# Last quarter of the output projection as one chunk of 512 columns, eight of its weight tiles resident, and a rewritten layer boundary

## The chip, the core and the metric

The kernel runs on one core of a Trainium2 chip. The metric is the device time of one execution in microseconds (us). TensorE multiplies matrices, VectorE and ScalarE do elementwise work, GpSimd does some elementwise work and issues some DMAs, and SyncE issues most DMAs. In profiles they are PE (PEld for its weight loads), DVE, ACT, POOL and SP.

## The reference

Two layers run one after the other on x, 256 tokens by 2048 columns, all in float32. Per layer:

```
h = rms_norm(x, g_pre)
p = h @ w_in                         # 2048 -> 5952 columns
A: 8 query heads, 2 key/value heads, per-head RMS norm, 2-D rotary, softmax attention
B: 4 heads with low-rank q and kv, shared rotary key
C: 4 heads, neighbourhood attention on a 4 x 64 token grid with a learned bias
o = concat(A, B, C) * silu(gate columns of p)
y = o @ w_out                        # 2048 -> 2048
x = x + rms_norm(y, g_post)
```

What matters here is the last two lines of layer 0 and the first line of layer 1: y must be complete along its 2048 columns before its root mean square, and so the new x, is known; and layer 1's projection needs the new x times its norm weight, transposed.

## The kernel before, in words

Every matmul has 128 x 128 stationary operands. A float32 factor is kept as two parts, `hi` (a rounded copy) and `lo` (the rest), and a product is three matmuls: hi x hi, hi x lo, lo x hi (`mm3`, L219). The weights stream: they lie in memory as a list of items of up to 128 x 1024 float32 (512 KB). For each item SyncE loads a `raw` tile (`load`, L262; 4 buffers), ScalarE writes `hi`, VectorE writes `lo` by a subtraction (`conv`, L272, through `split`, L196; 5 buffers of each), and TensorE uses it (`products`, L852). `feed` (L283) keeps loads and conversions ahead of use: a conversion runs up to 4 items ahead, and not further than 5 tiles past the last item that is done with.

Items are grouped in chunks of output columns (`_chunks`, L43). For a layer's input projection the other factor is `hT`, the transposed x, also as hi and lo, one tile of 128 x 16 x 2 x 256. For the output projection it is `oT`, the gated attention output (one tile of hi, one of lo). A chunk of lay-out "T" has the token halves m = 0 and m = 1 (128 tokens each) as two PSUM tiles, and its columns are the moving dimension. The output projection y consists of y0, y1, y2 with 512 columns and y3, y4 with 256 columns; an item holds two k-tiles of 512 columns or four of 256.

As a chunk of y ends, ScalarE takes its sum of squares (`junk`, L338) and VectorE multiplies it by `g_post` (L740). The last chunk, y4, is run by `last_chunk` (L935), where the order is written out by hand: all items for m = 0, then, while TensorE runs the same items for m = 1, the end of the first half: `ends` gives the scale `rs_r` (VectorE `rs_a`, L957; a power on GpSimd, L958), `x_new` gives the residual (`residual`, L767, VectorE, four instructions of 512 columns) and the product with the next layer's norm weight (`x_gain`, L772, GpSimd, four instructions), `x_transpose` transposes it on TensorE (L225, four 128 x 128 blocks to a PSUM tile `tr`, two buffers), and `x_split` writes it as hi (ScalarE) and lo (VectorE) to `hT`. Behind y4 stand the items C[0] to C[5] of layer 1's first chunk (320 columns, three k-tiles to an item, 960 columns): first for m = 0, with the second half's chain in between, then for m = 1. In layer 1 the function writes the residual to the output instead and ends.

The framework schedules instructions by priority and dependences, so an engine's order need not be that of the text; the orders shown below are those of the built programs. Each engine runs its own order strictly and waits on semaphores.

## Time and profile before

| | us |
|---|---|
| median of 3 runs | 825.32 (824.39 to 826.72) |
| profiled execution | 826.01 |
| its span, first to last instruction | 824.2 |
| TensorE busy | 806.8 (98%) |
| VectorE busy | 557.2 (68%) |
| ScalarE busy | 436.7 (53%) |
| GpSimd busy | 52.6 (6%) |
| granted TensorE clock, mean | 0.993 |

An engine's busy time counts its instructions' spans; matmuls overlap and their ends are modelled, so for TensorE the distance between starts tells more than the span of one. A row of the timeline has start, length, engine, line, operation, destination and sources, count, and in brackets the idle time before it with what released it. Times are counted from the first instruction. Layer 0's y2 runs to about 384.9 us, y3 and y4 to 410, and the first chunk of layer 1 to about 433.6.

### The profile page before, as it was taken

Reading aid. Unit: us, or ns where it says so; the run is one execution under the profiler, and the core shown is the slowest. Engines: PE = TensorE matmul, PEld = TensorE weight load, DVE = VectorE, ACT = ScalarE, POOL = GpSimd, SP = SyncE. Lnnn points to the kernel's source line nnn. Section 1 sums busy time; section 2 is a strip of 40 time slices with the busy share of each in tenths; the row PEclk is TensorE's granted clock in tenths of the full one; section 3 lists DMA queues with packets and bytes.
Section 4 is the critical chain, followed back from the end, with each engine's and each line's share of the span. In section 5 each row is a group of like instructions: output and inputs, shape, how many; then the busy total and the mean of one; then the engine's idle time right before and its main releaser. Section 6 shows DMA issues by size and latency. Waiting matters only on the chain.

```text
span 824.2 us, 12380 instructions
## 1 busy us (share of the span) xinstructions
PE 806.8 (98%) x4659; PEld 711.6 (86%) x4659; DVE 557.2 (68%) x871; ACT 436.7 (53%) x765; POOL 52.6 (6%) x63
## 2 busy tenths in 40 slices
PE   8999999999999999999989999999999999999996
PEld 5999888888888888888888998888889888888896
DVE  6567777476786687554686667875767866874544
ACT  6574555454665565454454455655456555554440
POOL 1110000000000000200340000000000000000000
PEclk9999999999999999999989999999999999999998
DMA  8875544654545466665347546446545454556632
GB/s 296 293 290 191 195 164 154 226 189 172 180 144 189 152 209 207 233 230 184 136 180 246 167 167 204 156 151 231 192 163 179 154 180 163 195 199 213 201 130 102
DMA packets 46235, 156.72 MB, mean 190 GB/s; under 512 B 5216, under 2 KB 7392, under 8 KB 46176
## 3 DMA queue, kind: packets, MB, share of 16 engines
q1 hardware_dynamic: 43584, 146.50, 51.7%
q0 software_dynamic: 2592, 9.44, 3.3%
q8 instruction: 36, 0.59, 0.3%
q14 instruction: 23, 0.19, 0.1%
HBM read 151.72 MB, written 4.19 MB: 189 GB/s over the span
## 4 chain that ended last, share of the span: by engine, by line
PE 78%; issue 12%; DVE 3%; DMA 3%; POOL 1%; ACT 1%; SPq 1%; DVEq 0%; POOLq 0%; ACTq 0%
PE mm L216 64%; PE pv L216 5%; PE sc L216 5%; PE tr L225 3%; DVE wlo L201 2%; DMA wraw<-in_wts_dram 1%; DMA u<-in_x_dram 1%; DMA g_akn<-in_akn_dram 1%; PE tr L216 1%; DVE u L767 1%; ACT whi L200 1%; DVE hT L204 0%; ACT junk L338 0%; POOL rs_r L212 0%; POOL s_akn L315 0%
## 5 line engine op out<-in xcount | busy, mean ns | idle before, releaser
L201 DVE TENSOR_TENSOR wlo<-wraw,whi 128x1024 fp32r<-128x1024 f32 (+2 forms) x265 | 321.4, 1215 | 186.8 <-ACT whi L200 182.0
L200 ACT CAST whi<-wraw 128x1024 fp32r<-128x1024 f32 (+2 forms) x265 | 273.4, 1033 | 247.2 <-PE mm L216 202.1
L216 PE MATMUL mm<-whi,hT 128*128 128x512 f32 (+1 forms) x768 | 234.5, 380 | 4.8 <-DVE hT L201 3.5
L216 PEld LDWEIGHTS mm<-whi,hT 128*128 128x128 f32 x768 | 143.1, 190 | 30.6 <-DVE hT L201 3.8
L216 PE MATMUL mm<-whi,oT 128*128 128x512 f32 (+1 forms) x640 | 166.8, 348 | 0.0
L216 PE MATMUL mm<-hT,whi 128*128 128x512 f32 x640 | 161.1, 393 | 0.0
L216 PE MATMUL mm<-wlo,hT 128*128 128x512 f32 (+1 forms) x384 | 145.6, 380 | 0.9 <-DVE wlo L201 0.9
L216 PEld LDWEIGHTS mm<-hT,whi 128*128 128x128 f32 x640 | 115.2, 189 | 20.8
L216 PEld LDWEIGHTS mm<-whi,oT 128*128 128x128 f32 x640 | 112.2, 189 | 14.8
L216 PE MATMUL mm<-wlo,oT 128*128 128x512 f32 (+1 forms) x320 | 108.9, 347 | 0.0
L216 PEld LDWEIGHTS mm<-hT,wlo 128*128 128x128 f32 x640 | 87.3, 190 | 6.3
L216 PE MATMUL mm<-hT,wlo 128*128 128x256 f32 x640 | 89.2, 282 | 0.0
L216 PEld LDWEIGHTS mm<-wlo,hT 128*128 128x128 f32 x384 | 72.8, 190 | 14.1 <-DVE wlo L201 2.6
L216 PEld LDWEIGHTS mm<-wlo,oT 128*128 128x128 f32 x320 | 60.6, 189 | 7.3
L216 PE MATMUL sc<-u,u 128*128 128x256 f32 x224 | 33.7, 290 | 0.0
L212 POOL TENSOR_TENSOR rs_r<-rs_a,mhalf 128x2 f32<-128x2 f32 (+2 forms) x12 | 15.1, 1256 | 281.4 <-DVE rs_a L211 281.4
L678 ACT ACTIVATE pr<-sc,nb,scq 128x256 f32<-128x256 f32 x32 | 17.8, 560 | 25.3 <-DVE nb L673 25.3
L216 PEld LDWEIGHTS sc<-u,u 128*128 128x128 f32 x224 | 29.1, 190 | 0.5
L216 PE MATMUL pv<-pT,u 128*128 128x256 f32 x192 | 28.1, 282 | 0.0
L216 PEld LDWEIGHTS pv<-pT,u 128*128 128x128 f32 x192 | 26.2, 189 | 1.3
L216 PE MATMUL pv<-hT,whi 128*128 128x256 f32 x128 | 23.7, 285 | 0.0
L338 ACT ACTIVATE junk<-mm 128x512 bf16<-128x512 f32 (+1 forms) x20 | 10.2, 508 | 24.8 <-PE mm L216 24.7
(140 smaller groups left out, 763.7 us busy)
## 6 DMA issues: line engine op xcount, KB each, us to landing
wraw<-in_wts_dram SPq DMA_DIRECT2D x247, 512.0 KB, 3.8
wraw<-in_wts_dram SPq DMA_DIRECT2D x10, 480.0 KB, 4.3
u<-in_x_dram SPq DMA_DIRECT2D x4, 512.0 KB, 8.6
u<-in_bias_dram POOLq DMA_DIRECT2D x4, 512.0 KB, 5.0
u<-in_x_dram POOLq DMA_DIRECT2D x4, 512.0 KB, 5.5
u<-in_gpost_dram POOLq DMA_DIRECT2D x4, 512.0 KB, 6.4
x<-u SPq DMA_DIRECT2D x4, 512.0 KB, 2.8
u<-x POOLq DMA_DIRECT2D x4, 512.0 KB, 5.2
```

The lines of the kernel that those rows point to most:

```text
L200: nc.scalar.copy(hi.bitcast(F32R), ps)
L201: nc.vector.tensor_tensor(lo.bitcast(F32R), ps, hi, ALU.subtract)
L212: nc.gpsimd.tensor_tensor(r[:, :m], a[:, :m], self.mhalf[:, :m], ALU.pow)
L216: self.nc.tensor.matmul(out, lhsT=l.bitcast(F32R), rhs=r.bitcast(F32R), start=start, stop=stop, skip_group_check=True)
L225: self.nc.tensor.transpose(out, in_, self.ident)
L338: self.nc.scalar.activation(j[:, :n], src, AF.Square, scale=scale, accum_out=acc)
L678: nc.scalar.activation(pr[:, qt], s3[:, qt], AF.Exp, bias=nb[:, qt:qt + 1], scale=scale, accum_out=sm[:, qt:qt + 1])
L767: self.nc.vector.scalar_tensor_tensor(xc, self.q4(self.yg[m], c), r[:, :1], xc, ALU.mult, ALU.add)
```

## The change

y3 and y4 become one chunk y3 of 512 columns, eight items of two k-tiles. It is now the chunk that `last_chunk` runs, so eight items are used for m = 0 and again for m = 1. `hT` becomes four tiles hT0 to hT3 of 128 x 2048, each holding four k-tiles. Items 0 to 3 of y3 are held: their hi and lo go into these four tiles, which get layer 1's transposed x afterwards. The other items use the usual buffers, and `feed` counts only these ("place"); during y2 it converts up to four items further ahead. `x_gain` runs on VectorE instead of GpSimd. In `last_chunk` the first half's residuals, products, transposes and splits are spread over the eight items of the second pass, and the conversions of layer 1's items are placed by `conv(j)`. `post_y3` is gone, `post_y2` makes the partial sum `ypre` of three chunks, and y3's sum of squares is the fourth.

```diff
--- before
+++ after
@@ -25,6 +25,7 @@
 LO_BUFS = 5
 WARM = 11
 LC = 4
+HELD = 4
 HEAD_EVERY = {"A": 4, "B": 4, "C": 3}
 
 
@@ -72,8 +73,7 @@
         ("y0", "T", "out", np.arange(0, 512), 2),
         ("y1", "T", "out", np.arange(512, 1024), 2),
         ("y2", "T", "out", np.arange(1024, 1536), 2),
-        ("y3", "T", "out", np.arange(1536, 1792), 4),
-        ("y4", "T", "out", np.arange(1792, 2048), 4),
+        ("y3", "T", "out", np.arange(1536, 2048), 2),
     ]
 
 
@@ -113,6 +113,12 @@
         i = own.index(y[0])
         late = [it for it in y if it["ks"][0] >= 12]
         order += own[:i] + [it for it in y if it not in late] + late + own[i + len(y):]
+    place = 0
+    for it in order:
+        j = it["ks"][0] // 2
+        it["held"] = j if it["name"] == "y3" and j < HELD else None
+        it["place"] = place
+        place += it["held"] is None
     return order, off
 
 
@@ -272,8 +278,12 @@
     def conv(self, i):
         it = self.items[i]
         n = it["ncols"]
-        hi = self.pw.tile([P, 1024], F32, tag="hi", name=self.nm("whi"), bufs=HI_BUFS)[:, :it["n"]]
-        lo = self.pw.tile([P, 1024], F32, tag="lo", name=self.nm("wlo"), bufs=LO_BUFS)[:, :it["n"]]
+        if it["held"] is not None:
+            t = self.h_slot(it["held"])
+            hi, lo = t[:, :1024], t[:, 1024:]
+        else:
+            hi = self.pw.tile([P, 1024], F32, tag="hi", name=self.nm("whi"), bufs=HI_BUFS)[:, :it["n"]]
+            lo = self.pw.tile([P, 1024], F32, tag="lo", name=self.nm("wlo"), bufs=LO_BUFS)[:, :it["n"]]
         n1 = n if i == 0 else it["n"]
         for c in range(0, it["n"], n1):
             self.split(it["raw"][:, c:c + n1], hi[:, c:c + n1], lo[:, c:c + n1])
@@ -283,15 +293,19 @@
     def feed(self, cur, done, lc=LC):
 
         n = len(self.items)
-        while self.nconv < min(n, cur + lc + 1, done + HI_BUFS):
-            while self.nload < min(n, self.nconv + RAW_BUFS):
-                self.load(self.nload)
-                self.nload += 1
-            self.conv(self.nconv)
-            self.nconv += 1
+        place = lambda i: self.items[i]["place"]
+        while self.nconv < min(n, cur + lc + 1) and place(self.nconv) < place(done) + HI_BUFS:
+            self.conv_next()
         while self.nload < min(n, self.nconv + RAW_BUFS):
             self.load(self.nload)
             self.nload += 1
+
+    def conv_next(self):
+        while self.nload < min(len(self.items), self.nconv + RAW_BUFS):
+            self.load(self.nload)
+            self.nload += 1
+        self.conv(self.nconv)
+        self.nconv += 1
 
 
     def layer_consts(self, l):
@@ -754,12 +768,9 @@
 
     def post_y2(self, l, ps):
         yield from self.post_y(l, ps, 2, 512, 2)
-
-    def post_y3(self, l, ps):
-        yield from self.post_y(l, ps, 6, 256, 3)
         self.ypre = self.tmp("ypre", [P, 2])
         for m in range(2):
-            self.nc.vector.reduce_sum(self.ypre[:, m:m + 1], self.yss[m][:, :4], AX.X)
+            self.nc.vector.reduce_sum(self.ypre[:, m:m + 1], self.yss[m][:, :3], AX.X)
         self.nc.vector.tensor_scalar(self.ypre, self.ypre, 1.0 / D, EPS, ALU.mult, ALU.add)
 
     def residual(self, m, c, r):
@@ -769,7 +780,7 @@
 
     def x_gain(self, m, c):
 
-        self.nc.gpsimd.tensor_tensor(self.q4(self.xg[m], c), self.q4(self.xt[m], c), self.q4(self.g_next, c), ALU.mult)
+        self.nc.vector.tensor_tensor(self.q4(self.xg[m], c), self.q4(self.xt[m], c), self.q4(self.g_next, c), ALU.mult)
 
     def x_transpose(self, m, c):
         xc = self.q4(self.xg[m], c)
@@ -780,10 +791,17 @@
 
     def x_split(self, m, c, pt):
         t = slice(m * P, (m + 1) * P)
-        self.split(pt.rearrange("p (k t) -> p k t", k=4), self.hT[:, 4 * c:4 * c + 4, 0, t], self.hT[:, 4 * c:4 * c + 4, 1, t])
+        self.split(pt.rearrange("p (k t) -> p k t", k=4), self.hT[c][:, :, 0, t], self.hT[c][:, :, 1, t])
 
     def new_h(self):
-        self.hT = self.pc.tile([P, KT, 2, 256], F32, tag="hT", name=self.nm("hT"))
+        self.hT = [self.h_part(c) for c in range(4)]
+
+    def h_slot(self, c):
+        return self.pc.tile([P, 2048], F32, tag=f"hT{c}", name=self.nm(f"hT{c}"))
+
+    def h_part(self, c):
+
+        return self.h_slot(c).rearrange("p (k h t) -> p k h t", k=4, h=2)
 
     def new_layer(self):
         self.new_h()
@@ -941,75 +959,109 @@
         self.open_chunk(self.items[i])
         ps = self.cur[l, self.items[i]["ci"]]
         n = self.items[i]["ncols"]
-        F = range(i, i + 4)
-        for f in F:
-            self.feed(f, i)
-            self.products(self.items[f], (0,))
+        F = [self.items[i + j] for j in range(8)]
+        for j in range(8):
+            self.feed(i + j, i)
+            self.products(F[j], (0,))
             self.run_tasks()
-        self.require((l, "y3"))
+        self.require((l, "y2"))
         rs = [None, None]
         self.xg = [None, None]
 
         def ends(m):
-            self.sumsq(ps[m][:, :n], self.yss[m][:, 4:5])
+            self.sumsq(ps[m][:, :n], self.yss[m][:, 3:4])
             rs[m] = self.tmp("rs_r", [P, 8], bufs=4)
             a = self.tmp("rs_a", [P, 8], bufs=2)
-            nc.vector.tensor_scalar(a[:, :1], self.yss[m][:, 4:5], 1.0 / D, self.ypre[:, m:m + 1], ALU.mult, ALU.add)
+            nc.vector.tensor_scalar(a[:, :1], self.yss[m][:, 3:4], 1.0 / D, self.ypre[:, m:m + 1], ALU.mult, ALU.add)
             nc.gpsimd.tensor_tensor(rs[m][:, :1], a[:, :1], self.mhalf[:, :1], ALU.pow)
-            self.times_gain(ps, m, 7, n)
-
-        def x_new(m):
+            self.times_gain(ps, m, 3, n)
             if more:
                 self.xg[m] = self.unit(5 - 5 * m)
-            for c in range(4):
+
+        def x_new(m, *cs):
+            for c in cs:
                 xc = self.residual(m, c, rs[m])
                 if more:
                     self.x_gain(m, c)
                 else:
                     nc.sync.dma_start(self.out[m][:, c * 512:(c + 1) * 512], xc)
 
+        pt = {}
+
+        def turn(m, c):
+            pt[m, c] = self.x_transpose(m, c)
+
+        def take(m, c):
+            if m == 0:
+                self.hT[c] = self.h_part(c)
+            self.x_split(m, c, pt[m, c])
+
+        def f(j):
+            self.products(F[j], (1,))
+
         ends(0)
-        for f in F:
-            if f == i + 1:
-                x_new(0)
-            if more and f == i + 3:
-                self.new_h()
-                for c in range(2):
-                    self.x_split(0, c, self.x_transpose(0, c))
-            self.products(self.items[f], (1,))
-            if more and f == i:
-                self.feed(f + 4, f + 1)
+        f(0)
+        x_new(0, 0, 1)
+        f(1)
+        f(2)
         if not more:
+            x_new(0, 2, 3)
+            for j in range(3, 8):
+                f(j)
             ends(1)
-            x_new(1)
+            x_new(1, 0, 1, 2, 3)
             return
+        c0 = i + 8
+        C = [self.items[c0 + j] for j in range(6)]
+
+        def conv(j):
+            if self.nconv == c0 + j:
+                self.conv_next()
+            assert self.nconv > c0 + j
+
+        conv(0)
+        turn(0, 0)
+        x_new(0, 2)
+        f(3)
+        turn(0, 1)
+        take(0, 0)
+        take(0, 1)
+        f(4)
+        turn(0, 2)
+        x_new(0, 3)
+        f(5)
+        take(0, 2)
+        conv(1)
+        f(6)
+        turn(0, 3)
+        take(0, 3)
+        conv(2)
+        f(7)
         if l == 0:
             self.x1 = [self.tc.dram_tile([P, 2048], F32, name=f"x1_{m}") for m in range(2)]
-        c0 = i + 4
-        C = [self.items[c0 + j] for j in range(6)]
         self.open_chunk(C[0])
         self.new_o()
         ends(1)
-        self.feed(c0 + 2, c0, 0)
+        conv(3)
         self.products(C[0], (0,))
-        pt = [self.x_transpose(0, 2), self.x_transpose(0, 3)]
-        self.x_split(0, 2, pt[0])
-        x_new(1)
+        x_new(1, 0, 1)
         self.products(C[1], (0,))
-        self.feed(c0 + 3, c0, 0)
-        self.x_split(0, 3, pt[1])
         self.products(C[2], (0,))
-        self.feed(c0 + 4, c0, 0)
+        conv(4)
+        x_new(1, 2)
         self.products(C[3], (0,))
-        pt = [self.x_transpose(1, 0), self.x_transpose(1, 1)]
-        self.x_split(1, 0, pt[0])
-        self.x_split(1, 1, pt[1])
+        turn(1, 0)
+        turn(1, 1)
+        take(1, 0)
+        take(1, 1)
+        x_new(1, 3)
         self.products(C[4], (0,))
-        pt = [self.x_transpose(1, 2), self.x_transpose(1, 3)]
+        turn(1, 2)
+        take(1, 2)
         self.products(C[0], (1,))
-        self.x_split(1, 2, pt[0])
-        self.x_split(1, 3, pt[1])
-        self.feed(c0 + 5, c0 + 1, 0)
+        turn(1, 3)
+        conv(5)
+        take(1, 3)
         self.products(C[1], (1,))
         self.products(C[5], (0,))
         for j in range(2, 6):
@@ -1028,11 +1080,12 @@
         while i < n:
             self.step += 1
             it = self.items[i]
-            if it["name"] == "y4":
+            if it["name"] == "y3":
                 self.last_chunk(i)
-                i += 10
+                i += 14
                 continue
-            self.feed(i, i)
+
+            self.feed(i, i, LC + min(HELD, it["ks"][0] // 2) if it["name"] == "y2" else LC)
             if it["first"]:
                 self.open_chunk(it)
             self.products(it)
```

The first place is VectorE's order from the first half's first residual to the second half's scale (`rs_a`). Of the names, `u` tiles are residual x, products and norm weights, `wlo` a layer 1 item's lo part, `hT` the transposed x's lo part, `rs_a` the mean square of a half. Before:

```order
L767 SCALAR_TENSOR_TENSOR u_748_3696<-u_744_3692,rs_r_4086,u_748_3696 128x512 x2
L767 SCALAR_TENSOR_TENSOR u_749_3697<-u_745_3693,rs_r_4086,u_749_3697 128x512
L201 TENSOR_TENSOR wlo_4104<-wraw_3929,whi_4103 128x960
L767 SCALAR_TENSOR_TENSOR u_749_3697<-u_745_3693,rs_r_4086,u_749_3697 128x512
L201 TENSOR_TENSOR wlo_4186<-wraw_3962,whi_4185 128x960
L201 TENSOR_TENSOR wlo_4232<-wraw_3992,whi_4231 128x960
L201 TENSOR_TENSOR hT_4143<-tr_4144,hT_4143 128x4x128
L201 TENSOR_TENSOR hT_4143<-tr_4151,hT_4143 128x4x128
L957 TENSOR_SCALAR rs_a_4181<-yss_757_3713,ypre_4080 128x1
```

After:

```order
L778 SCALAR_TENSOR_TENSOR u_751_3699<-u_747_3695,rs_r_3981,u_751_3699 128x512 x2
L783 TENSOR_TENSOR u_813_3986<-u_751_3699,u_757_3705 128x512 x2
L778 SCALAR_TENSOR_TENSOR u_752_3700<-u_748_3696,rs_r_3981,u_752_3700 128x512 x2
L783 TENSOR_TENSOR u_814_3987<-u_752_3700,u_758_3706 128x512
L207 TENSOR_TENSOR hT_817_4028<-tr_4010,hT_817_4028 128x4x128
L783 TENSOR_TENSOR u_814_3987<-u_752_3700,u_758_3706 128x512
L207 TENSOR_TENSOR hT_818_4031<-tr_4023,hT_818_4031 128x4x128
L207 TENSOR_TENSOR wlo_4057<-wraw_3863,whi_4056 128x960
L207 TENSOR_TENSOR hT_820_4053<-tr_4040,hT_820_4053 128x4x128
L207 TENSOR_TENSOR wlo_4077<-wraw_3881,whi_4076 128x960
L207 TENSOR_TENSOR wlo_4106<-wraw_3899,whi_4105 128x960
L207 TENSOR_TENSOR hT_824_4071<-tr_4066,hT_824_4071 128x4x128
```

Before, four residuals and three conversions stand ahead of the first two `hT` subtractions, and the products are not on this engine. Now each pair of residuals is followed by its products, all four `hT` subtractions of the first half stand here (the next row is the second half's `rs_a`), and the conversion that stood between the residuals comes behind them. The lines are those of the changed file: L778 is the residual, L783 the product, L207 the subtraction in `split`.

The second place is TensorE's order in the second half's pass over the last items. `mm_4019` and `mm_3914` are the second half's PSUM tile, `whi`, `wlo` and the last row group's `hT_786`, `hT_788` weight items, `oT` the stationary factor, `tr` the transposes of the first half's x. Before:

```order
L216 MATMUL mm_4019<-whi_3958,oT_15_117 128x256 x4
L225 MATMUL tr_4144<-ident,u_821_4109 128x128 x4
L225 MATMUL tr_4151<-ident,u_821_4109 128x128 x4
L216 MATMUL mm_4019<-whi_3988,oT_14_116 128x256
L216 MATMUL mm_4019<-wlo_3989,oT_14_116 128x256
```

After:

```order
L222 MATMUL mm_3914<-hT_786_3831,oT_17_119 128x512 x4
L222 MATMUL mm_3914<-hT_786_3831,oT_18_120 128x512 x2
L231 MATMUL tr_4010<-ident,u_813_3986 128x128 x4
L222 MATMUL mm_3914<-hT_788_3836,oT_17_119 128x512 x4
L222 MATMUL mm_3914<-hT_788_3836,oT_18_120 128x512 x2
L231 MATMUL tr_4023<-ident,u_813_3986 128x128 x4
L222 MATMUL mm_3914<-whi_3841,oT_17_119 128x512
L222 MATMUL mm_3914<-wlo_3842,oT_17_119 128x512
```

Before, two groups of transposes stand ahead of the last of four items (its first two rows are shown), and behind that item comes layer 1's first matmul. Now the first group stands ahead of the fourth of eight items, and one group stands ahead of each of the fourth, fifth, sixth and eighth. Items 0 to 3 are read from `hT` tiles.

## Rows read from the trace of the kernel before

**Rows 1.** The page: engines' busy us; ScalarE's costliest group (busy us, mean ns).

```profile
PE 806.8 (98%) x4659; PEld 711.6 (86%) x4659; DVE 557.2 (68%) x871; ACT 436.7 (53%) x765; POOL 52.6 (6%) x63
...
L200 ACT CAST whi<-wraw 128x1024 fp32r<-128x1024 f32 (+2 forms) x265 | 273.4, 1033 | 247.2 <-PE mm L216 202.1
```

**Rows 2.** The list of waits of PE: us in total, times, longest.

```profile
PE mm L216 <- DVE hT L201: 3.5, 1, 3.5
...
PE tr L225 <- POOL u L772: 1.0, 1, 1.0
```

**Rows 3.** Busy time of each engine, granted clock, DMA share and GB/s by stretch.

```profile
10.00:20.00 10.00, 9.34 (x39) 6.87 (x38) 9.92 (x16) 9.28 (x17) 0.00 (x0) 1.00 0.90 337
...
363.10:384.90 21.80, 21.80 (x97) 18.03 (x97) 11.09 (x10) 9.74 (x13) 0.00 (x0) 1.00 0.58 194
...
402.20:412.00 9.80, 7.90 (x64) 7.38 (x62) 8.70 (x9) 6.19 (x11) 7.25 (x5) 1.00 0.24 86
412.00:420.50 8.50, 5.83 (x23) 5.79 (x24) 7.57 (x10) 3.72 (x11) 4.53 (x5) 0.60 0.57 213
```

**Rows 4.** Timeline of PE where y2 passes into y3.

```profile
381.05 0.39 PE L216 MATMUL mm<-wlo,oT 128*128 128x512 f32 x1
...
381.73 0.39 PE L216 MATMUL mm<-wlo,oT 128*128 128x512 f32 x1
...
385.02 0.28 PE L216 MATMUL mm<-wlo,oT 128*128 128x256 f32 x1
...
385.38 0.28 PE L216 MATMUL mm<-wlo,oT 128*128 128x256 f32 x1
```

**Rows 5.** Timeline of PE at the layer boundary.

```profile
408.15 0.66 PE L225 MATMUL tr<-ident,u 128*128 128x128 f32 x4 [1.02 <-POOL u L772]
...
414.67 1.17 PE L216 MATMUL mm<-whi,hT 128*128 128x320 f32 x3 [3.55 <-DVE hT L201]
...
418.14 0.47 PE L216 MATMUL mm<-wlo,hT 128*128 128x320 f32 x1
418.41 0.47 PE L216 MATMUL mm<-whi,hT 128*128 128x320 f32 x1
...
422.75 1.03 PE L225 MATMUL tr<-ident,u 128*128 128x128 f32 x8
423.54 0.39 PE L216 MATMUL mm<-whi,hT 128*128 128x320 f32 x1
```

**Rows 6.** Timeline of PE at the end of layer 1's first chunk.

```profile
430.64 0.31 PE L216 MATMUL mm<-wlo,hT 128*128 128x320 f32 x1
...
431.96 0.31 PE L216 MATMUL mm<-wlo,hT 128*128 128x320 f32 x1
...
433.81 0.39 PE L216 MATMUL mm<-wlo,hT 128*128 128x512 f32 x1
```

**Rows 7.** Timeline of ACT: sums of squares of 512 and of 256 columns.

```profile
384.43 0.60 ACT L338 ACTIVATE junk<-mm 128x512 bf16<-128x512 f32 x1 [0.98 <-PE mm L216]
...
402.44 0.38 ACT L338 ACTIVATE junk<-mm 128x256 bf16<-128x256 f32 x1 [4.39 <-PE mm L216]
```

**Rows 8.** Timeline of DVE, then of POOL, at the first half's chain.

```profile
403.85 3.12 DVE L767 SCALAR_TENSOR_TENSOR u<-u,rs_r,u 128x512 f32<-128x512 f32 x3 [0.35 <-POOL rs_r L958]
...
404.68 5.58 POOL L772 TENSOR_TENSOR u<-u,u 128x512 f32<-128x512 f32 x3 [0.86 <-DVE u L767]
```

**Rows 9.** Groups of DVE from 402.2 to 433.6 us (busy, mean ns of one).

```profile
L767 DVE SCALAR_TENSOR_TENSOR u<-u,rs_r,u 128x512 f32<-128x512 f32 x8 | 8.8, 1136 | 0.8 <-POOL rs_r L958 0.8
L201 DVE TENSOR_TENSOR wlo<-wraw,whi 128x960 fp32r<-128x960 f32 x4 | 7.2, 1808 | 0.0
L201 DVE TENSOR_TENSOR hT<-tr,hT 128x512 fp32r<-128x512 f32 x8 | 5.2, 682 | 1.3 <-ACT hT L200 1.3
```

**Rows 10.** Timeline of DVE with POOL idle: a conversion, and layer 1's residuals.

```profile
397.71 1.16 DVE L201 TENSOR_TENSOR wlo<-wraw,whi 128x960 fp32r<-128x960 f32 x1 [0.40 <-ACT whi L200]
...
812.32 2.74 DVE L767 SCALAR_TENSOR_TENSOR u<-u,rs_r,u 128x512 f32<-128x512 f32 x4 [0.35 <-POOL rs_r L958]
```

More of the change, by code (lines that the diff above doesn't have):

```diff
@@ L731, in y_tiles @@
                 nc.gpsimd.dma_start(self.xt[m][i], (self.x if l == 0 else self.x1)[m][:, sl])
-        self.yss = [self.tmp(f"yss{m}", [P, 5]) for m in range(2)]
+        self.yss = [self.tmp(f"yss{m}", [P, 4]) for m in range(2)]
     def take_y(self, ps, m, c, n, j):
@@ L839, in src @@
             return self.cqT(k)
-        return self.ckvT(k) if w == "ukv" else self.hT[:, k]
+        return self.ckvT(k) if w == "ukv" else self.hT[k // 4][:, k % 4]
     def open_chunk(self, it):
@@ L928, in start @@
                 k = 4 * c + j
-                self.split(v[:, j], self.hT[:, k, 0], self.hT[:, k, 1], self.g_pre[:, k:k + 1])
+                self.split(v[:, j], self.hT[c][:, j, 0], self.hT[c][:, j, 1], self.g_pre[:, k:k + 1])
                 if j % 2:
```

## Prediction, made before the changed kernel was run

> **What bounds the kernel now.** I read the totals first. TensorE is busy in 98% of the span [rows 1], so a change of the time must shorten TensorE's work or the little idle time it has. The list of TensorE's waits for the whole run shows where that idle time lies: the two longest entries that are not the start of the program are 3.5 us behind VectorE's `hT` and 1.0 us behind GpSimd's `u` [rows 2]. The timeline puts both at the layer boundary, at 414.67 and 408.15 us [rows 5]. The reader is to see there that the long wait costs more than itself. Before it a matmul of 320 columns starts every 0.147 us (nine from 430.64 to 431.96, undisturbed [rows 6]); after it they start every 0.27 us (418.14, 418.41), and the granted clock of 412 to 420.5 us is 0.60 [rows 3, 5], that is, partly the lower level of 1.2 GHz. Last I read what feeds the boundary: VectorE is busy 8.70 of 9.80 us between 402.2 and 412 us [rows 3], and beside GpSimd's products its own instructions are slow: a residual 1.136 us and a `wlo` of 960 columns 1.808 us [rows 9], against 0.685 (2.74 for four) and 1.16 where GpSimd is idle [rows 10].
>
> **The boundary in one number.** The last 512 columns of y begin at 384.90 us (0.12 before 385.02 [rows 4]) and the first chunk of layer 1 ends at 433.58 (0.23 before 433.81 [rows 6]): 48.7 us. Work in it: 192 matmuls of 256 columns at 0.120 us (three from 385.02 to 385.38 [rows 4]) = 23.0; 32 transposes at 0.099 (eight from 422.75 to 423.54 [rows 5]) = 3.2; 96 matmuls of 320 columns at 0.147 = 14.1. Sum 40.3. So 8.4 us are lost: 1.0 and 3.5 of waits, some 2.7 to the lower clock (matmuls and transposes from 414.67 to 420.5 at about twice their start-to-start time), and 1.2 at the seams, where a wait begins under the modelled end of the last matmul or is too short to be listed.
>
> **The change part by part.**
>
> *Wider matmuls.* A matmul of 512 columns starts every 0.227 us (three from 381.05 to 381.73 [rows 4]). 96 of them take 21.76 us where 192 took 23.04: 1.28 us off in each layer, on TensorE, which is the path: 2.56. By the rows a matmul costs 0.013 us beyond its columns (0.120 x 2 - 0.227). The Trainium skill, page "TensorE: Matmul & The Clock Gate", section "Wait — 56ns, not 53.3ns?", gives about 2.5 ns for that cost on a warm array; by it 192 matmuls fewer save 0.5 us. The rows measure both widths in this very program, so the sum keeps 2.56.
>
> *Eight items resident.* Both halves of the rows now pass over eight split tiles, so the eight must exist when the first pass is over, and ideally before its items come up every 1.36 us. Four sit in hT's place, free since the last input chunk; their conversions are spread over y2. The other four and the first of layer 1 use the ordinary tiles, freed as y2's items end, 2.72 us apart, the last at 384.9, when item 7 is still 9.5 us from its turn. From 363.1 to 384.9 ScalarE is busy 9.74 and VectorE 11.09 of 21.8 us [rows 3]; four more conversions at 1.03 us on ScalarE [rows 1] and 1.24 on VectorE (1.16 for 960 columns [rows 10], scaled to 1024) leave both near or under 16. Loads rise by 4 x 0.52 MB, from 194 to 290 GB/s in that stretch; from 10 to 20 us the queue moved 337 [rows 3]. I cost it at nothing. If the cover were gone the items would come at the conversion's pace of about 1.2 us, still under 1.36; a late DMA would cost at most about 2.
>
> *First half's chain.* Count from the end of the first pass, t = 0. In the kernel before the sum of squares starts 0.26 later and the first residual 1.41 after that (402.44 to 403.85 [rows 7, 8]); with 512 columns the ACTIVATE takes 0.60 instead of 0.38 [rows 7], so the first residual starts at 1.9. VectorE then does residual, residual, product, product, and so on. The product is new there: the nearest row is the `hT` subtraction of the same 512 columns, 0.682 us [rows 9]; bounds 0.60 (half of a 960-column one) and 1.86 (what GpSimd took, 5.58 for three [rows 8]). I take 0.68, since it is the same engine and size. The first product ends at 1.9 + 1.37 + 0.68 = 3.95. TensorE does three items (4.08) before the first transposes: no wait, or 0.2. The second product ends at 4.6 (wanted 5.9), the third at 6.6 (7.7), the fourth at 7.9 (10.9). TensorE's second pass with 16 transposes ends at 12.5. The 1.0 us wait goes, and the 3.5 us wait goes: `hT` of the first chunks is split at about 7 to 8, long before layer 1's first matmul at 12.5.
>
> *VectorE meanwhile.* Four residuals 2.7, four products 2.7, four `hT` 2.7, three `wlo` of 960 columns 3.5 = 11.7 us against 12.5 of TensorE. It starts at 1.9, and the conversions of layer 1's items 1 to 3 wait for tiles that the second pass frees (items 4 to 6, the last at about 10.9), so it is through at about 13.9. It no longer shares the stretch with GpSimd: eight residuals 0.45 and four `wlo` 0.65 shorter = 6.2 us, about what the eight products (5.4) bring [rows 9, 10].
>
> *Second half's chain.* The scale row of the second half stands behind that queue: 13.9 instead of 13.5. Residuals from 14.8, the first two products done at 17.5. TensorE meanwhile does four items of layer 1 for the first half, 4 x 1.32, to 17.8: no wait. The fifth `wlo` ends at 18.6, just when it is wanted. The third product ends at 20.7 and the split that frees the transposes' PSUM tile at 21.3, while TensorE is there at 20.5: a wait of 0.8. The fourth costs 0.3. I take 1.0 for both, bounds 0 and 3; waits of this size lowered no clock before (the 1.0 us one at 408.15 lies in a stretch at 1.00). Boundary after: 21.8 + 3.2 + 14.1 + 1.0 = 40.0, against 48.7: 8.7 off, the 1.28 included.
>
> *Layer 1's end.* 1.28 off in the matmuls; the tail behind the last matmul is 0.22 longer (the wider sum of squares). The wider gain (0.68 for 0.42) lies beside GpSimd's power. Net 1.1 off.
>
> **Sum.** 8.7 + 1.1 = 9.8. The profiled execution took 826.0, so 816.2; the three timed runs have a median 0.7 lower, so 815.5. I predict 815.9, between them.
>
> **Rivals.**
> 1. *VectorE stays slow in this stretch.* The slow residuals and `wlo` would be a matter of the stretch, not of GpSimd. For it: it is the busiest helper there. Against it: the same instructions take 0.685 and 1.16 where GpSimd is idle [rows 10]. Then VectorE needs 16.7 instead of 11.7; TensorE waits 1.1 for the first transposes, 4.9 for the second half's, loses 2.7 to the clock and 1.0 elsewhere: 9.7 where 8.4 were lost. Against 2.3 from the wider matmuls that leaves 1.0: 824.7. The Trainium skill, "Perfetto Trace Analysis", section "Optimizing Scalar/DVE Operations", says that with a saturated VectorE offloading to ScalarE or even GpSimd may make sense, which speaks against the move; it adds that GpSimd and VectorE share a port, so that moving work between these two might not help. The trace shows the second half of that rule (1.808 against 1.16).
> 2. *The other side: the product also takes GpSimd's 1.86 us on VectorE.* Place: the four instructions ahead of each half's first transposes. VectorE's queue is then 20 us; TensorE waits 1.9, then about 9, loses 2.7 and 0.3: 13.9 lost, 5.5 more than now, less 2.3: 829. It decides once the waits exceed 10.7 us in all, that is, VectorE's instructions about 1.6 times as long as I take them. Against it: no 512-column VectorE row without GpSimd beside it is near that.
> 3. *Half the wait comes back.* Layer 1's conversions wait on ScalarE for tiles of the second pass and stand ahead of the `hT` casts in its strict order; with each of the three handovers 1 us later than I have it, TensorE loses 3.5 more: 819.4. For it: the margins at the second half are 0.1 to 0.4 us.
> 4. *The matmul's fixed cost is that of the page.* 0.5 instead of 2.56: 818.0. Against it the pitches of rows 4.
>
> **Chances.** Forecast 0.80, rival 1 0.05, rival 2 0.03, rival 3 0.10, rival 4 0.02. A measurement of this kernel tells about 0.3% (2.5 us) from no change. Faster by more: 0.80 + 0.10 + 0.02, less a little for a mix of 1 and 3: 0.91; within: 0.06; slower: 0.03. The range starts where no wait at all is left and the fastest run is the base (824.4 - 8.4 - 2.3 = 813.7) and reaches to rival 3 and its like: 813.7 to 819.8. The forecast's own range is 813.7 to 818.
>
> **What would show it.** Right: matmuls of y3 at 0.227 us in both passes; no PE wait over 1 us between y2 and layer 1; the granted clock 1.00 through the boundary; 39 to 41 us from y2's end to the end of layer 1's first chunk; residuals near 0.69 and products near 0.68 on VectorE; the tail after the last matmul 0.2 longer. Wrong: gaps in y3's first pass (conversion or loads too late); a wait at the first transposes (the product's price) or at the second half's (VectorE's queue); a clock below 1.00 there, which would add over 2 us.

## The result, and the profile after

| | median (us) | lowest to highest | ratio to before, 95% interval |
|---|---|---|---|
| before | 825.05 | 824.39 to 826.72 | |
| changed | 816.68 | 815.02 to 817.51 | 0.9883 [0.9861, 0.9904] |

The changed kernel is 8.4 us faster by the medians and 9.7 by the ratio; 815.9 us was forecast. Its profiled execution took 816.09 us, its span is 814.3 us where it was 824.2.

The page first: engines' busy us and ScalarE's costliest group. It answers to [rows 1].

```profile
PE 802.2 (99%) x4467; PEld 698.5 (86%) x4467; DVE 555.4 (68%) x875; ACT 435.8 (54%) x757; POOL 37.6 (5%) x55
...
L206 ACT CAST whi<-wraw 128x1024 fp32r<-128x1024 f32 (+2 forms) x257 | 265.0, 1032 | 227.4 <-PE mm L222 175.7
```

TensorE has 192 matmuls fewer and GpSimd 15 us less to do. The list of TensorE's waits over the whole run (us in total, times, longest) answers to [rows 2]:

```profile
PE tr L231 <- DVE rbc L850: 1.5, 1, 1.5
PE pv L918 <- DVE rs_a L938: 1.3, 1, 1.3
PE mm L222 <- DVE wlo L207: 1.1, 3, 0.5
PE mm L222 <- ACT whi L206: 0.2, 1, 0.2
```

The two waits of the boundary, 3.5 and 1.0 us, are off the list; what is left lies elsewhere. The windows (length; busy us and count of PE, PEld, DVE, ACT and POOL; granted clock, DMA share, GB/s) cover y2, the first pass of y3, the second pass with its transposes, four items of layer 1, and the rest of that chunk; they answer to [rows 3].

```profile
363.00:384.90 21.90, 21.90 (x98) 18.13 (x97) 14.77 (x13) 13.23 (x16) 0.00 (x0) 1.00 0.73 245
384.90:395.80 10.90, 10.90 (x50) 9.02 (x49) 3.79 (x7) 2.39 (x6) 0.00 (x0) 1.00 0.51 171
395.80:408.40 12.60, 12.60 (x65) 10.39 (x64) 10.54 (x16) 5.83 (x9) 0.56 (x1) 1.00 0.26 98
408.40:413.80 5.40, 5.40 (x38) 5.36 (x37) 5.26 (x9) 4.86 (x12) 0.56 (x1) 1.00 0.82 265
413.80:424.70 10.90, 10.84 (x78) 10.44 (x77) 10.28 (x24) 8.71 (x19) 1.31 (x3) 1.00 0.55 197
```

TensorE is busy in every one, at a granted clock of 1.00, the upper level; before, it was busy 5.83 of 8.50 us at 0.60 in the worst stretch. TensorE's timeline there (start, us, operation, count) answers to [rows 4 to 6].

```profile
384.91 5.60 PE L222 MATMUL mm<-hT,oT 128*128 128x512 f32 x24
...
395.79 4.25 PE L222 MATMUL mm<-hT,oT 128*128 128x512 f32 x18
399.87 0.60 PE L231 MATMUL tr<-ident,u 128*128 128x128 f32 x4
...
413.83 1.03 PE L231 MATMUL tr<-ident,u 128*128 128x128 f32 x8
...
416.83 0.65 PE L231 MATMUL tr<-ident,u 128*128 128x128 f32 x4
...
424.97 0.40 PE L222 MATMUL mm<-wlo,hT 128*128 128x512 f32 x1
```

The first pass takes 10.88 us (384.91 to 395.79: 48 matmuls, 0.227 us each) and no transposition waits. From y2's end to the end of layer 1's first chunk (0.23 before 424.97) it is 39.83 us, where it was 48.7. VectorE's groups from 395.8 to 424.7 us (busy us, mean ns, idle before) answer to [rows 9]:

```profile
L778 DVE SCALAR_TENSOR_TENSOR u<-u,rs_r,u 128x512 f32<-128x512 f32 x8 | 5.6, 746 | 0.2
L207 DVE TENSOR_TENSOR hT<-tr,hT 128x512 fp32r<-128x512 f32 x8 | 5.4, 685 | 0.2
L783 DVE TENSOR_TENSOR u<-u,u 128x512 f32<-128x512 f32 x8 | 5.3, 684 | 0.0
L207 DVE TENSOR_TENSOR wlo<-wraw,whi 128x960 fp32r<-128x960 f32 x4 | 4.6, 1157 | 1.0 <-ACT whi L206 0.9
```

With GpSimd all but idle, a residual costs 0.75 instead of 1.14 us, a `wlo` 1.16 instead of 1.81, and the new product 0.68. Layer 1's end, on VectorE (the answer to [rows 10]):

```profile
807.30 0.21 DVE L975 TENSOR_SCALAR rs_a<-yss,ypre 128x1 f32<-128x1 f32 x1 [6.95 <-ACT junk L352]
807.43 0.68 DVE L754 TENSOR_TENSOR u<-mm,u 128x512 f32<-128x512 f32 x1
808.24 2.74 DVE L778 SCALAR_TENSOR_TENSOR u<-u,rs_r,u 128x512 f32<-128x512 f32 x4
```

The tail's sum of squares starts at 806.57, 7.73 us before the span ends, against 7.53 before (816.67 of 824.2): 0.20 longer. The sum closes. From the boundary's end to this sum of squares it is 381.83 us (424.74 to 806.57), where it was 383.09 (433.58 to 816.67): 1.26 less. Boundary 8.85 and layer 1's end 1.26 - 0.20 make 9.9, the difference of the two spans.

### The profile page after: what moved, and what is told of

It is laid out like the page before. It is cut to its first block, busy times and chain, and to the rows that moved or that the text cites. A ratio compares the mean times of both kernels' runs of the same rounds, so it can differ in the third digit from the quotient of the medians.

```text
span 814.3 us, 11966 instructions
## 1 busy us (share of the span) xinstructions
PE 802.2 (99%) x4467; PEld 698.5 (86%) x4467; DVE 555.4 (68%) x875; ACT 435.8 (54%) x757; POOL 37.6 (5%) x55
## 4 chain that ended last, share of the span: by engine, by line
PE 95%; DVE 2%; DMA 1%; ACT 1%; SPq 0%; issue 0%; DVEq 0%; POOLq 0%; POOL 0%; ACTq 0%
PE mm L222 80%; PE sc L222 6%; PE pv L222 6%; PE tr L231 3%; DMA u<-in_xT_dram 1%; DVE wlo L207 1%; PE tr L222 1%; DVE u L778 1%; ACT whi L206 0%; ACT hT L209 0%; DVE u L783 0%; SPq L274 0%; SPq L923 0%; DVE hT L207 0%; DVEq L1136 0%
## 5 line engine op out<-in xcount | busy, mean ns | idle before, releaser
L207 DVE TENSOR_TENSOR wlo<-wraw,whi 128x1024 fp32r<-128x1024 f32 (+2 forms) x257 | 309.0, 1204 | 168.2 <-ACT whi L206 165.0
L206 ACT CAST whi<-wraw 128x1024 fp32r<-128x1024 f32 (+2 forms) x257 | 265.0, 1032 | 227.4 <-PE mm L222 175.7
L222 PE MATMUL mm<-whi,oT 128*128 128x512 f32 x448 | 141.6, 391 | 0.0
L222 PEld LDWEIGHTS mm<-whi,oT 128*128 128x128 f32 x448 | 84.1, 188 | 17.1
L222 PE MATMUL mm<-wlo,oT 128*128 128x512 f32 x224 | 87.2, 389 | 0.0
L222 PEld LDWEIGHTS mm<-wlo,oT 128*128 128x128 f32 x224 | 42.1, 188 | 8.4
L352 ACT ACTIVATE junk<-mm 128x512 bf16<-128x512 f32 x16 | 9.5, 593 | 32.6 <-PE mm L222 32.6
```

The costliest lines, as they stand in the source:

```text
L206: nc.scalar.copy(hi.bitcast(F32R), ps)
L207: nc.vector.tensor_tensor(lo.bitcast(F32R), ps, hi, ALU.subtract)
L222: self.nc.tensor.matmul(out, lhsT=l.bitcast(F32R), rhs=r.bitcast(F32R), start=start, stop=stop, skip_group_check=True)
L352: self.nc.scalar.activation(j[:, :n], src, AF.Square, scale=scale, accum_out=acc)
```

## The experiments

The time came out, but three edits were made at once. Theory: each edit pays its own share of the boundary. Rival: they are different ways to one end, so that one does most of it and the rest little. To compare kernels I use one number, what the boundary loses: the time from y2's end to the end of layer 1's first chunk, less TensorE's own work there (39.1 us with the wide chunk, 40.3 with two narrow ones, as the prediction counted). Before it is 8.4, after 0.7. Each such number is read from one profiled execution. Ratios are to the kernel before on the same chip, with a 95% interval; the runs were spread over several chips, so ratios compare two of them better than medians do.

**The product back on GpSimd** (all else as changed).

```diff
-        self.nc.vector.tensor_tensor(self.q4(self.xg[m], c), ...
+        self.nc.gpsimd.tensor_tensor(self.q4(self.xg[m], c), ...
```

> The changed kernel with the products with the norm weight back on GpSimd. My account: a product takes 1.3 to 1.86 us there, the first one ends 4.5 us after the first pass (wanted 4.1), each later one 1.86 after the last, so TensorE waits 0.4 to 0.8 us at the first half and 1 to 1.5 at the first transposes of the second half, and VectorE's residuals and lo parts beside GpSimd take about 1.1 and 1.8 us, which delays the second half's scale: 2 to 3.5 us slower than the changed kernel (816.7), 818.5 to 820, clock still 1.00. Rival, the order alone carries the gain and GpSimd's product is covered: 816 to 817. Rival, the products' engine carries it: the 3.5 us wait and the clock come back, 822 or more.

Measured 819.27 us, ratio 0.9916 [0.9894, 0.9938]; lost 3.2 us. TensorE's waits in the boundary:

```profile
PE tr L231 <- POOL u L783: 1.2, 2, 0.9
PE tr L231 <- DVE hT L207: 0.4, 1, 0.4
PE mm L222 <- DVE wlo L207: 0.4, 1, 0.4
```

As expected: the product's place is worth 2.5 us of the boundary once all the rest is there. VectorE is slow beside GpSimd again (eight residuals, mean ns in the last but one column):

```profile
L778 DVE SCALAR_TENSOR_TENSOR u<-u,rs_r,u 128x512 f32<-128x512 f32 x8 | 8.6, 1131 | 0.2
```

**The product alone, on the kernel before**: the same edit the other way round.

> The kernel before with the products on VectorE and nothing else changed. My account: the 1.0 us wait goes (both products end before the transposes are wanted), VectorE's queue ahead of layer 1's first matmul is 2.7 us of products longer but 2 to 4 us of slowing by GpSimd shorter, so the 3.5 us wait shrinks to about 2.4 and the clock may stay up: 820 to 823 against 825. Rival, VectorE is full and the products push it over: 825 or more. Rival, the products' engine carries the gain: 819 or less.

Measured 826.38 us, ratio 0.9988 [0.9974, 1.0002]; lost 7.9. My expectation failed: nothing is gained. TensorE's waits in the boundary:

```profile
PE mm L216 <- DVE wlo L201: 1.7, 1, 1.7
PE tr L225 <- DVE u L772: 1.4, 2, 0.8
PE mm L216 <- ACT hT L200: 0.7, 1, 0.7
```

The reader is to see that the 3.5 us wait behind the first half's `hT` has become shorter ones; three of the four, from 415.93 to 420.04 us, stand behind layer 1's first items. The granted clock still falls, to 0.72 in this window (the clock is third from the right):

```profile
413.80:425.00 11.20, 8.09 (x39) 7.32 (x38) 9.28 (x16) 5.18 (x14) 0.65 (x3) 0.72 0.65 234
```

The first half's chain is shorter (VectorE reaches the second half's scale at 411.25 instead of 415.13 us), but the second half's residuals and products now stand in one queue, from 413.77 to 418.83 us, and the `wlo` behind which TensorE waits 1.7 us comes only after it.

**The old order at the boundary**, with the wide chunk and eight resident items; once with VectorE's product, once with GpSimd's as before (that is, the wide held chunk alone).

```diff
         ends(0)
         f(0)
-        x_new(0, 0, 1)
-        f(1)
-        f(2)
...
         conv(0)
...
+        f(1)
+        x_new(0, 0, 1, 2, 3)
+        for j in range(2, 6):
+            f(j)
         conv(1)
+        for c in range(2):
+            turn(0, c)
+            take(0, c)
         f(6)
-        turn(0, 3)
-        take(0, 3)
-        conv(2)
         f(7)
...
```

> The changed kernel (512 columns, held tiles, products on VectorE) with the boundary in the order of the kernel before: all four residuals and products first, two groups of transposes ahead of the last quarter of the second pass, the other two behind layer 1's first item, the second half's four residuals and products in one piece. My account: the first half has no wait, but the split of the last quarter of hT and the fifth conversion stand behind the whole second half's chain on VectorE; TensorE waits 2 to 3 us at the fifth item and 1 to 1.5 after it: 819.5 to 821. Rival, the longer second pass covers any order: 816 to 817.

> As the run before, with the products on GpSimd too: of the change only the 512 columns and the held tiles are left. My account: waits of 5 to 6 us at the second half's transposes and splits, perhaps with a lowered clock (2 to 3 us more): 821.5 to 824, so that the wide chunk by itself gives 1 to 3.5 us, not the whole 8.4. Rival, the longer second pass is what matters: 817 to 818.

Measured 818.53 us, 0.9897 [0.9875, 0.9919], lost 2.4 with VectorE's product; 817.22 us, 0.9891 [0.9870, 0.9911], lost 2.7 with GpSimd's. The first lies between its account (819.5 to 821) and its rival (816 to 817). The second is the surprise: 821.5 to 824 was expected. Its waits in the boundary, and its residuals:

```profile
PE tr L231 <- DVE hT L207: 1.3, 1, 1.3
PE mm L222 <- DVE wlo L207: 0.7, 1, 0.7
...
L778 DVE SCALAR_TENSOR_TENSOR u<-u,rs_r,u 128x512 f32<-128x512 f32 x8 | 9.1, 1189 | 0.2
```

VectorE's residuals are as slow there as before (the `wlo` of 960 columns takes 1.496 us, between 1.808 and 1.157), the order is the old one, and yet 5.7 of 8.4 us of the loss are gone. So the wide chunk with its eight resident items does most of it by itself.

With the long second pass these runs also part order and product: 2.7 us are lost with the old order and GpSimd's product, 2.4 with VectorE's product alone, 3.2 with the new order alone, 0.7 with both. Either alone gives next to nothing in these traces (0.3 and -0.5 us), both together give 2.0: the two need each other here, and the 2.5 us above is the product's worth beside the new order only.

By what does the wide chunk do it: its width, or the length of the second pass?

**The wide chunk with a short second pass.** Old order, GpSimd's product, 512 columns; only the last four items are worked half after half, so the second pass is 24 matmuls (5.4 us) and not 48.

```diff
-HELD = 4
+HELD = 0
...
-        F = [self.items[i + j] for j in range(8)]
-        for j in range(8):
-            self.feed(i + j, i)
+        for j in range(4):
+            self.feed(i + j, i + j)
+            self.products(self.items[i + j])
+            self.run_tasks()
+        F = [self.items[i + 4 + j] for j in range(4)]
+        for j in range(4):
+            self.feed(i + 4 + j, i + 4)
...
```

> The last chunk of y has 512 columns, but only its last four items are worked one token half after the other, as before: its first four run both halves at once, no split tile lies in hT's place, the order at the boundary and GpSimd's product are as before. So the second pass is some 5.5 us of TensorE work instead of 10.9. Theory (the long second pass, which eight resident items allow, carries the gain): the boundary waits of 4 us and more are back (before: 1.0 and 3.5 us, then a granted clock of 0.60), the stretch from the first pass to the end of the next chunk takes 46 us or more of the same work, and only the 2.5 us of 192 matmuls fewer in both layers remain: 822.5 to 825. Rival (the width itself, with half as many matmuls to feed, carries it): waits of about 2 us at the boundary as in the two kernels with the old order, 816.5 to 819.

Measured 825.39 us, ratio 0.9985 [0.9972, 0.9999]; lost 10.2. The theory held, 0.4 us above its range, and the rival fell. Waits in the boundary, and windows:

```profile
PE mm L222 <- DVE wlo L207: 3.6, 1, 3.6
PE mm L222 <- DVE hT L207: 2.5, 1, 2.5
PE tr L231 <- POOL u L783: 1.3, 2, 1.0
```

```profile
402.00:412.00 10.00, 7.10 (x36) 5.42 (x34) 9.65 (x8) 6.51 (x12) 7.82 (x5) 1.00 0.32 121
412.00:425.00 13.00, 8.50 (x51) 8.21 (x52) 12.50 (x17) 6.99 (x18) 8.99 (x8) 0.89 0.49 171
```

It is the picture of before: VectorE all but full, TensorE waiting for each of its products in turn, the clock below 1.00. The width alone is worth its 192 matmuls and no more, and most of these is eaten here by the boundary, which loses 1.8 us more than before.

**Six resident items**, between the two, with the old order and GpSimd's product.

```diff
-HELD = 4
+HELD = 2
...
-        for j in range(8):
-            self.feed(i + j, i)
+        for j in range(2):
+            self.feed(i + j, i + j)
+            self.products(self.items[i + j])
+            self.run_tasks()
+        F = [self.items[i + 2 + j] for j in range(6)]
+        for j in range(6):
+            self.feed(i + 2 + j, i + 2)
...
```

> Between the two kernels with the old order and GpSimd's product: six of y3's eight items are worked half after half (second pass 36 matmuls of 0.227 us = 8.2 us, against 5.4 with four and 10.9 with eight), two split tiles lie in hT's place, everything else as with four and as with eight. From the end of y2 to the first matmul of 512 columns after the boundary the kernel with four lost 10.4 us beyond TensorE's own 39.1, the one with eight 2.7. Theory (the second pass is cover, and each microsecond less of it is a microsecond more of waits, with a dearer clock on top): 6 to 7 us lost there, 820 to 822. Rival (there is a point from which the chain is covered, and six items are past it): 3 to 4 us lost, no granted clock below 1.00 in the boundary, 817.5 to 819.

Measured 819.9 us, ratio 0.9935 [0.9917, 0.9953]; lost 5.3, between theory and rival. With the old order, four, six and eight items lose 10.2, 5.3 and 2.7 us: the first 2.7 us of cover take away 4.9, the next 2.6. (The 10.4 in this expectation counts to the second matmul of the next chunk.) The clock has a part in the first step, which gives more than it is long; how large a part isn't shown. With four items it fell to 0.89, with six it stays at 1.00 in every window of the boundary, with 1.3 us as the longest wait.

**The short pass with the new order and VectorE's product.** The same four items, all else as changed.

```diff
-HELD = 4
+HELD = 0
...
         f(2)
...
         turn(0, 0)
         x_new(0, 2)
-        f(3)
         turn(0, 1)
         take(0, 0)
         take(0, 1)
-        f(4)
+        f(3)
         turn(0, 2)
...
```

> The changed kernel with only four of y3's items worked half after half (second pass 5.4 us instead of 10.9, nothing in hT's place), but with the new order at the boundary and VectorE's product: what order and product do without the length. With four items and the old order and product the boundary lost 10.2 us beyond TensorE's own 39.1. Theory (the length is what covers the chains; order and product only shape what is left): VectorE's 11.7 us of work for the first half no longer fits beside 5.4 us, TensorE waits for the second half's chain: 5 to 7 us lost, 820 to 822.5. Rival 1 (order and product cure the boundary by themselves, the length was only one way to the same end): under 3 us lost, 816.5 to 818.5. Rival 2 (without the length they do nothing, as the product alone did on the kernel before): 9 us or more lost, 824 to 826.

Measured 819.03 us, ratio 0.9922 [0.9903, 0.9941]; lost 3.6, better than my theory, short of rival 1. Waits in the boundary, and VectorE's timeline:

```profile
PE mm L222 <- DVE wlo L207: 0.8, 1, 0.8
PE tr L231 <- DVE u L783: 0.4, 1, 0.4
```

```profile
402.31 1.41 DVE L778 SCALAR_TENSOR_TENSOR u<-u,rs_r,u 128x512 f32<-128x512 f32 x2
403.65 1.28 DVE L783 TENSOR_TENSOR u<-u,u 128x512 f32<-128x512 f32 x2
404.85 1.41 DVE L778 SCALAR_TENSOR_TENSOR u<-u,rs_r,u 128x512 f32<-128x512 f32 x2
406.18 0.68 DVE L783 TENSOR_TENSOR u<-u,u 128x512 f32<-128x512 f32 x1
406.78 1.28 DVE L207 TENSOR_TENSOR hT<-tr,hT 128x512 fp32r<-128x512 f32 x2
```

VectorE splits the first two `hT` parts at 406.78, 6.1 us after the sum of squares (400.69). In the kernel with the old order and the same short pass these two rows stand behind four residuals of 1.2 us and two `wlo` of 2.2 us, 10.65 us after it (401.54):

```profile
403.16 4.79 DVE L778 SCALAR_TENSOR_TENSOR u<-u,rs_r,u 128x512 f32<-128x512 f32 x4
407.87 4.39 DVE L207 TENSOR_TENSOR wlo<-wraw,whi 128x960 fp32r<-128x960 f32 x2
412.19 1.27 DVE L207 TENSOR_TENSOR hT<-tr,hT 128x512 fp32r<-128x512 f32 x2
```

So these four corners answer the question; both theories had a part of it.

| lost in the boundary, us (time) | old order, GpSimd's product | new order, VectorE's product |
|---|---|---|
| second pass of 4 items | 10.2 (825.39) | 3.6 (819.03) |
| second pass of 8 items | 2.7 (817.22) | 0.7 (816.68) |

A longer cover gives 7.5 where the chain is long and 2.9 where it is short; a shorter chain gives 6.6 where the cover is short and 2.0 where it is long. They are substitutes: no fixed share of the 9.5 us from corner to corner belongs to either. (In the order of the table, line by line, y3 and the chunk behind the boundary start at 384.96 and 434.27 us, 384.11 and 426.78, 383.99 and 425.81, 384.91 and 424.74.) The last step, 2.0 us, is seen in the traces alone: the medians differ by 0.5 us and the ratios by 0.0008, well within their intervals. So the wide chunk with eight resident items, in the old order and with GpSimd's product, has all of the gain in time that these runs can tell. Order and product were not split further for the short pass on the wide chunk; on the narrow chunk the product alone gave 0.5 of 8.4.

**Every 512-column matmul of y as two of 256**, else as changed.

```diff
+    def mmy(self, w, out, l, r, start, stop):
+        if w != "out":
+            return self.mm(out, l, r, start, stop)
+        for h in range(2):
+            c = slice(256 * h, 256 * h + 256)
+            self.mm(out[:, c], l, r[:, c], start and h == 0, stop)
...
```

> The kernel after, with every matmul of the four chunks of y that reads 512 columns issued as two of 256: 768 more matmuls, the same columns, the same eight resident items and the same order. Forecast's account (0.227 us for 512 columns against 2 x 0.120 us, 13.3 ns for each matmul more): 10.2 us more, 826 to 827.5. Rival (2.5 ns fixed cost for each matmul, by the Trainium skill's page TensorE: Matmul & The Clock Gate, section 'Wait - 56ns, not 53.3ns?'): 1.9 us more, 818 to 819.

Measured 825.91 us, ratio 0.9999 [0.9986, 1.0012]: 9.2 us above the changed kernel's median (9.6 by the ratios), 12 to 12.5 ns for each of 768 matmuls. The forecast's account is right to a tenth, the rival's 1.9 us is not. The boundary itself loses 0.7 as in the changed kernel: the price is the matmuls', not a wait's.

**No further look-ahead of the conversions during y2.**

```diff
-            self.feed(i, i, LC + min(HELD, it["ks"][0] // 2) if it["name"] == "y2" else LC)
+            self.feed(i, i)
```

> The kernel after, but while y2 runs the conversions look ahead no further than elsewhere (4 items): the first of the eight resident items are split as late as any other. Theory (the conversions have room here: ScalarE and VectorE are busy 54 and 68 per cent of the span): no wait of over 0.5 us in y3's first pass, 816 to 817.5. Rival (eight items in a row at 24 matmuls of 0.227 us for two items each ask more than the split engines give, and TensorE waits for whi or wlo in y3's first pass): waits of 1 to 4 us there in layer 0 and again in layer 1, 818 to 824.

Measured 815.17 us, ratio 0.9873 [0.9855, 0.9891], and no wait in the boundary. The theory held, with a time just below its range: eight items are split in time without it. Since 815.17 is a little under the changed kernel's first median, both ran once more on one chip.

> The changed kernel itself, to be compared on one chip with the version without the further look-ahead: 816 to 817.5, boundary 39.8 us.

> The changed kernel without the conversions' further look-ahead during y2, once more and on the same chip as the changed kernel. Theory (the look-ahead does nothing for the time): no difference beyond 0.2 per cent. Rival (it costs: eight conversions and loads ahead of y2's own push others back): 1 to 2 us less than the changed kernel.

Measured 815.87 us, 0.9887 [0.9867, 0.9906] for the changed kernel, 815.48 us, 0.9875 [0.9854, 0.9895] without the look-ahead. Twice a little lower, both times within the intervals: the look-ahead gives nothing, and that it costs something isn't shown.

**The largest wait that is left**, layer 0's `rbc`: its copy out of PSUM issued right behind its transposes.

```diff
             self.transpose(pt[:, m * P:(m + 1) * P], dgs[m])
-        yield 1
         self.rbc = self.tmp("rbc", [P, 256])
```

> The kernel after, with one thing moved in layer 0: the VectorE copy of rbc out of PSUM is issued right behind its transposes, ahead of one wlo of 1.21 us. TensorE's longest wait that is left (1.5 us at 60.6 us, transposes of t for rbc's buffer) should shrink by about 1.2 us: 815 to 816, a ratio to the kernel before about 0.0015 lower than after's. Rival (the copy waits for something else, or the wlo that is now late is itself waited for): no difference or a wait for wlo of about the same length, 816.5 to 818.

Measured 815.90 us, ratio 0.9882 [0.9865, 0.9900]: no difference that can be told. The time lies in the expected range (815 to 816), but the shorter wait that was to give it isn't there. In its trace, which is of the slowest of its four executions (818.17 us), the wait isn't gone; it has another releaser and is longer:

```profile
PE tr L231 <- DVE t L346: 3.2, 1, 3.2
```

The copy now starts ahead of the `wlo` (60.91 us), but TensorE's next transposes wait for `t`, which VectorE works right behind it (61.24). How much of the 3.2 us is this and how much a late start of the whole chain (below) stays open.

## Why the prediction was right

*Wider matmuls, 1.28 us a layer*: right. The pitch is 0.227 us in both passes, and layer 1 up to its tail is 1.26 us shorter. Twice the 256-column cost was put at 13.3 ns a matmul, and the split matmuls cost 12 to 12.5. The Trainium skill's page "TensorE: Matmul & The Clock Gate", section "Wait — 56ns, not 53.3ns?", has 2.5 ns; the trace differs here.

*Eight items resident, at nothing*: right. y2's stretch has ScalarE at 13.23 and VectorE at 14.77 us of 21.9, under the 16 forecast. The loads came to 245 GB/s where 290 were forecast, and three conversions more, not four, fell into this stretch; even without the look-ahead no item came late.

*First half's chain*: right to a tenth. From the end of the first pass at 395.79 the first residual starts 1.88 later (1.9 forecast), the two first products run from 399.00 for 1.29 us, so the first of them ends near 399.65 (3.86 after the pass; 3.95 forecast), and the first transposes at 399.87 have no wait:

```profile
397.67 1.41 DVE L778 SCALAR_TENSOR_TENSOR u<-u,rs_r,u 128x512 f32<-128x512 f32 x2
399.00 1.29 DVE L783 TENSOR_TENSOR u<-u,u 128x512 f32<-128x512 f32 x2
```

*VectorE meanwhile*: right. The second half's scale row starts at 409.62 us, 13.83 after the first pass (13.9 forecast).

*The second half's chain, 1.0 us of waits*: too dear, and what came in its place is another term. The gaps at 416.83 and 418.11 us are some 0.2 and 0.1, too short to be listed. The larger part of the 0.7 us lies at seven places where TensorE goes from transposes back to matmuls: there the first matmul takes 0.08 to 0.09 us longer than its pitch, as here 0.23 instead of 0.147.

```profile
414.62 0.39 PE L222 MATMUL mm<-whi,hT 128*128 128x320 f32 x1
414.85 0.31 PE L222 MATMUL mm<-wlo,hT 128*128 128x320 f32 x1
```

The prediction has no term for these. That the boundary came to 39.83 where 40.0 was forecast is therefore in part luck. The layer's end came to 1.06 of 1.1.

*Rival 1, VectorE stays slow*: its condition failed (746 and 1157 ns). *Rival 2, a product of 1.86 us*: failed (684 ns). *Rival 3, half the wait comes back*: failed, no wait came back. *Rival 4, the smaller fixed cost*: failed by the split matmuls. The prices of the first two can't be followed from their rows: with the slow residuals and `wlo` of rival 1 VectorE's 11.7 us become 15.4, not 16.7, and with the slow products of rival 2 16.4, not 20. One reading was wrong too: of TensorE's waits before, the second longest behind the program's start was not the 1.0 us one but 1.7 us behind layer 0's `rbc`, at 62 us; the sum doesn't use it.

What the prediction didn't see is what its steps hang on. It follows one kernel in which the cover (12.5 us of TensorE's work), the order and the product are all in place, and doesn't ask which of them the two waits need. The runs show that cover alone leaves 2.7 us of lost time and order with product alone 3.6. My expectations behind the prediction, not its sum, paid for this: I gave the product alone 2 to 5 us on the kernel before (nothing that can be told, measured) and the old order with GpSimd's product waits of 5 to 6 us (2.7 lost in all). The fault, as far as these runs show it, was to price an edit by the wait that ends at it. A chain on ScalarE, VectorE and GpSimd stands against a stretch of TensorE's work; an edit counts by how far it shortens the one or lengthens the other, and only as long as the chain is the longer of the two. VectorE's slow rows beside GpSimd were likewise true as a reading and cheap as a cause: with eight resident items they return (1131 and 1189 ns for a residual) at 2.5 us in the new order and 0.3 in the old one.

The Trainium skill's page "Perfetto Trace Analysis", section "Optimizing Scalar/DVE Operations", warns that GpSimd and VectorE share a port, so that moving work between the two might not help. The trace agrees where the product alone was moved (0.9988); with the new order and the long pass the move gave 2.5 us of the boundary, with the old order and the long pass 0.3.

## What to carry to other kernels

Where an engine waits at a boundary, write down two lengths: the chain that has to run there, and the independent work that the waiting engine has to do meanwhile. Lengthening the work (here by keeping more operands resident, so that one half's results are finished a whole pass before they are needed) and shortening or reordering the chain are substitutes; once one had brought the two lengths together, a third or so of its worth was left for the other here. Two edits of one chain can also need each other, as order and product did here. Of several edits at one place, run each alone and all but each: the sums of both kinds differ from the total, and that difference says which of them would have been enough. Here, in time, the wide chunk with its resident items would have been.

## What the runs showed of the hardware

The boundary itself repeats to the tenth: in five profiled executions with the changed boundary (the changed kernel twice, without the look-ahead twice, with the early `rbc`) it takes 39.83 to 39.85 us. What differs between them lies elsewhere.

Beside GpSimd's products VectorE's instructions don't all slow down. Residuals take 1.13 to 1.19 instead of 0.75 us and a `wlo` of 960 columns 1.43 to 1.90 instead of 1.16; the `hT` subtraction, which reads PSUM, takes 0.68 with and without.

In layer 0, near 60 us, TensorE waits for `rbc`, 0.9 to 3.3 us by kernel and execution. The chain behind it starts with a load of x. In the kernel with the old order and VectorE's product, ScalarE's timeline has:

```profile
43.32 0.63 ACT L352 ACTIVATE junk<-u 128x512 bf16<-128x512 f32 x1 [1.42 <-DMA u<-in_x_dram]
```

and in the changed kernel:

```profile
41.96 0.63 ACT L352 ACTIVATE junk<-u 128x512 bf16<-128x512 f32 x1 [0.44 <-DMA u<-in_x_dram]
```

There ScalarE waits 1 us longer for the load, and TensorE's wait for `rbc` is 3.3 instead of 1.5 us. That the one makes the other isn't shown: with six resident items ScalarE waits 0.94 us for the load, and TensorE only 1.1 for `rbc`. Behind the long wait TensorE's clock goes; the windows with the old order and VectorE's product (the clock stands third from the right):

```profile
60.00:64.00 4.00, 0.70 (x4) 0.62 (x4) 4.00 (x13) 1.29 (x3) 0.00 (x0) 0.78 0.90 291
64.00:68.00 4.00, 4.00 (x21) 4.00 (x20) 3.45 (x10) 0.94 (x3) 0.00 (x0) 0.50 0.67 217
```

A clock of 0.50 is the lower level, 1.2 GHz: 21 matmuls from 64 to 68 us where the changed kernel, after its 1.5 us wait, has 37 at 1.00. The length of the wait alone doesn't decide it: behind the same wait the clock stays at 1.00 after 2.7 us (the product alone on the kernel before), and falls to 0.77 from 64 to 68 us after 1.8 (the split matmuls). The execution with the old order and VectorE's product took 821.54 us against a median of 818.53. The boundary is steady now, so what varies here is the next place to look.
